# A down projection with two kinds of row-block pairs: the order in which its work is issued is written out and pinned

## The chip, the cores and the metric

The kernel runs on one core of one Trainium2 chip. The metric is the device time of one execution in microseconds (us). Three runs of the kernel before took 1710.01, 1710.61 and 1711.74 us; the median is 1710.61 us.

In the profile, PE is TensorE (matmuls; PEld its weight loads), DVE is VectorE, ACT is ScalarE, POOL is GpSimd and SP is SyncE, whose queue issues nearly all the DMAs. L102 is line 102 of the kernel.

## The reference, cut to what matters

One layer over 256 positions of width 2048: three gated attention branches, an output projection and a residual add, then a gated MLP. Only the end of the MLP is touched by the change:

```python
    h2 = _rmsnorm(x, ffn_norm)
    u = _causal_dwconv(h2 @ w_up, conv_w, conv_b)
    g, val = jnp.split(u, 2, axis=-1)
    return x + (jax.nn.silu(g) * val) @ w_down
```

`w_down` is 5504 x 2048 in float32, that is 43 row blocks of 128 rows.

## The kernel before, in words

**Float32 out of two parts.** Every matmul operand is split into a high part (an ACT copy into fp32r) and a low part (DVE: the value minus its high part). A product of two operands is three matmuls: high by high, high by low, low by high. Activations are split once; weights are split as they stream in. A weight tile is `raw` (128 x 1024, 512 KB, one DMA on SP's queue, 4 buffers), its high part is `whi` and its low part `wlo` (3 buffers each). `w_raw` (L155 holds its DMA) takes the tiles in one fixed order, `w_tiles` (L165, L166) splits them.

**The down projection.** The output is made in two halves of 1024 columns. In a half there are four cells: two blocks of 128 positions (`tt`) by two blocks of 512 columns (`h`). Two PSUM tiles `cc[0]` and `cc[1]` (pool `pj`, 2 buffers) hold the cells of one `tt` each. Row blocks are multiplied in two ways:

- A single block (`eight`): per cell three matmuls of 512 columns, so 12 matmuls.
- A pair of blocks (`seven`): the four blocks of a 2 x 2 product are made from seven products instead of eight (Strassen's scheme in Winograd's form), so 21 matmuls. Three of the products go straight into cells; the other four accumulate in four PSUM tiles `p1`, `p5`, `p6`, `p7` over all such pairs of the half. On the weight side a pair needs four differences of 128 x 512 (DVE, into `t`, L892 to L895), the high and low part of the first block's first 512 columns (`ha`, `la`), those of the second block (`hb`, `lb`), and the high and low parts of the four differences (`thl`, two at a time, L900 and L901). On the activation side three sums per pair (`sx`) are made while the up projection runs. The pairs that are done so are listed in `SEVEN`: 2, 3, 5, 7, 8, 10, 12, 13, 15, 17 (pair p holds blocks 2p and 2p+1); the other 23 blocks are single.

After the last pair of `SEVEN`, `gather` (L917 to L927) adds the four accumulators into `e`, the half's residual rows, which were loaded from DRAM (L861): one ACT copy of `p6` and seven DVE additions. The last three blocks (`TAIL`) are held until all three are split, and are then multiplied cell by cell; after each cell `store` (L929 to L932) adds it into `e` on DVE and issues the DMA to the output, on SP's queue for `tt` = 0 and on ACT's for `tt` = 1. In the last half the last cell is done in two pieces of 256 columns.

**What sets the order.** The engines run in parallel and each runs its own instructions in the order in which they were issued to it. That order isn't the order of the program text: a scheduler at build time picks, for every engine, the instruction with the highest priority among those that it takes to be ready. Priority is the order of the text, but instructions inside `tc.high_priority()` (the splits and differences of the weights) come ahead. Buffers of a pool are given out by it too; an instruction that needs a buffer waits for the last reader of its previous content.

Of the kernel before, what the change touches and what calls it, by code (L numbers as in the profile page):

```python
# [11 lines left out]
F32 = mybir.dt.float32  # L12
F32R = mybir.dt.float32r
# [27 lines left out]

SEVEN = (2, 3, 5, 7, 8, 10, 12, 13, 15, 17)
TAIL = 3


# [41 lines left out]
def hybrid_block(ctx: ExitStack, tc: tile.TileContext, x, xT, mem, memT, pos, inv, prm, gqk, bg, wts, out):  # L89
# [712 lines left out]
    with ExitStack() as fctx:  # L802
# [2 lines left out]
        sx = ap_.tile([P, len(SEVEN), 3, 2, P], F32R, name="sx")  # L805
        uctx = ExitStack()
        up = uctx.enter_context(tc.tile_pool(name="up", bufs=2))
        for c0 in range(0, NFF, 2):
            nb = min(2, NFF - c0)
            conv = []  # L810
            for half in range(2):
                ps = proj_cols(x2c, "up", KD, half * DFF + c0 * P, nb * P)
                u = up.tile([P, 2, T + 2], F32, name="u", bufs=3)
                nc.gpsimd.memset(u[:, :, 0:2], 0.0)
                uv = u[:, :nb, 2:]
                nc.scalar.activation(uv, ps[:, :nb, 1, :], AF.Copy)
# [31 lines left out]
        def mm3(o, l, r, start, stop):  # L848

            mm(o, l[0], r[0], start, False)  # L850
            mm(o, l[0], r[1], False, False)
            mm(o, l[1], r[0], False, stop)

        def hl(t):
            return t[:, 0, :], t[:, 1, :]

        for c0 in range(0, D, 1024):
            last = c0 + 1024 == D
            e = dn.tile([P, 2, 2, 512], F32, name="e")
            for tt in range(2):  # L860
                nc.sync.dma_start(e[:, tt], x2d[tt * P:(tt + 1) * P, c0:c0 + 1024])  # L861
            cc = [pj.tile([P, 2, 512], F32, name="pj") for _ in range(2)]
            p1, p5, p6, p7 = (pa.tile([P, 512], F32, name=nm, bufs=nb) for nm, nb in
                              (("t", 1), ("s", 2), ("s", 2), ("o", 1)))
            begun = set()

            def add(key, o, l, r, stop):
                mm3(o, l, r, key not in begun, stop)
                begun.add(key)

            def eight(k, hi, lo, cells, cols=(0, 512)):
                for tt, h in cells:
                    r = tuple(w[:, h * 512 + cols[0]:h * 512 + cols[1]] for w in (hi, lo))
                    add((tt, h), cc[tt][:, h, cols[0]:cols[1]], hl(fc[:, k, :, tt * P:(tt + 1) * P]), r,
                        k == NFF - 1)

            cells = [(tt, h) for tt in range(2) for h in range(2)]

            def seven(p):
                a, b = 2 * p, 2 * p + 1  # L880
                i, end = SEVEN.index(p), p == SEVEN[-1]
                ra, rb = (w_raw("down", k, c0, 1024)[0] for k in (a, b))
# [6 lines left out]
                with tc.high_priority():  # L889
                    nc.scalar.activation(ha[:, :512], b11, AF.Copy)  # L890
                    nc.scalar.activation(hb, rb, AF.Copy)
                    nc.vector.tensor_sub(t[:, 0], b12, b11)  # L892
                    nc.vector.tensor_sub(t[:, 1], b12, b22)  # L893
                    nc.vector.tensor_sub(t[:, 2], b22, t[:, 0])
                    nc.vector.tensor_sub(t[:, 3], b21, t[:, 2])  # L895
                    nc.vector.tensor_sub(la[:, :512], b11, ha[:, :512].bitcast(F32))
                    nc.vector.tensor_sub(lb, rb, hb.bitcast(F32))
                    for q in range(2):
                        th, tl = tq[:, 0, 2 * q:2 * q + 2], tq[:, 1, 2 * q:2 * q + 2]
                        nc.scalar.activation(th, t[:, 2 * q:2 * q + 2], AF.Copy)  # L900
                        nc.vector.tensor_sub(tl, t[:, 2 * q:2 * q + 2], th.bitcast(F32))  # L901
                step()
# [6 lines left out]
                add("p1", p1, a11, w11, end)  # L909
                add((0, 0), cc[0][:, 0], a12, w21, False)  # L910
                add((0, 1), cc[0][:, 1], s4, w22, False)
                add("p5", p5, s1, w1, end)
                add("p7", p7, s3, w3, end)
                add("p6", p6, s2, w2, end)
                add((1, 0), cc[1][:, 0], a22, w4, False)

            def gather():  # L917

                u = wraw.tile([P, 1024], F32, name="raw")[:, :512]
                nc.vector.tensor_add(e[:, 0, 0], e[:, 0, 0], p1)  # L920
                nc.scalar.activation(u, p6, AF.Copy)
                nc.vector.tensor_add(u, u, p1)
                for tt in range(2):
                    nc.vector.tensor_add(e[:, tt, 1], e[:, tt, 1], p5)
                nc.vector.tensor_add(e[:, 0, 1], e[:, 0, 1], u)
                nc.vector.tensor_add(u, u, p7)
                nc.vector.tensor_add(e[:, 1], e[:, 1], u.unsqueeze(1).to_broadcast([P, 2, 512]))  # L927

            def store(tt, a, b):  # L929
                d = e[:, tt].rearrange("p h n -> p (h n)")[:, a:b]  # L930
                nc.vector.tensor_add(d, d, cc[tt].rearrange("p h n -> p (h n)")[:, a:b])  # L931
                (nc.sync, nc.scalar)[tt].dma_start(out[tt * P:(tt + 1) * P, c0 + a:c0 + b], d)  # L932

            for p in range((NFF - TAIL) // 2):
                if p in SEVEN:
                    seven(p)
                    if p == SEVEN[-1]:
                        gather()
                else:
                    for k, hi, lo in w_tiles("down", 2 * p + 2, c0, 1024, 2 * p):  # L940
                        eight(k, hi, lo, cells)
            rest = list(w_tiles("down", NFF, c0, 1024, NFF - TAIL))
            for tt, h in cells:
                if last and (tt, h) == cells[-1]:
                    for a in (0, 256):
                        for k, hi, lo in rest:
                            eight(k, hi, lo, [(tt, h)], (a, a + 256))
                        store(tt, h * 512 + a, h * 512 + a + 256)
                else:
                    for k, hi, lo in rest:  # L950
                        eight(k, hi, lo, [(tt, h)])
                    store(tt, h * 512, h * 512 + 512)


_ORDER = ["x", "xT", "mem", "memT", "pos", "inv", "prm", "gqk", "bg", "wts"]
# [39 lines left out]
```

## Time and profile before

| | |
|---|---|
| time, median of 3 runs | 1710.61 us (1710.01 to 1711.74) |
| profiled execution | 1710.57 us, its span 1708.8 us |
| DVE, ACT, POOL busy | 1175.5, 897.0, 6.9 us |
| DMA | 332.78 MB, mean 195 GB/s |
| weight tiles | 586 DMAs of up to 512 KB on SP's queue, 3.4 us to landing (median of the 581 full ones) |
| down projection, first to last matmul | 1457.47 to 1705.4 us of the span |
| splitting a tile of 1024 columns | ACT 1057 ns, DVE 1220 ns (means of 549) |

How to read it: "busy" is the time in which an engine worked, as a share of the span. A line of a group names the source line, engine, operation, what it writes and reads, and the count; behind the bar come busy time and the mean of one, and behind a second bar the idle time just before them with what ended it. In the timeline a row has start, duration, engine, line, operation and tiles; brackets at its end give the idle time before it and what released it. Rows that follow each other may be merged (x2, x3).

### The profile page before, as it was taken

The page shows a single profiled execution, that of the slowest core. Times are in us where ns is not written, and L with a number is a line of the kernel's source. Part 1 is how long each engine was busy: PE and PEld are TensorE (multiplying, and loading weights), DVE is VectorE, ACT ScalarE, POOL GpSimd, SP SyncE. Part 2 cuts the span into 40 slices and gives each one's busy share as a digit, 9 for nine tenths or more (in the row PEclk, how much of TensorE's full clock was granted, in tenths as well). Part 3 has the DMA queues.
Part 4 walks back from the last instruction along what each step waited for, and adds up shares of the span by engine and source line. Part 5 has one row for each costly group of instructions (what it writes and reads, how often), then busy time and mean ns, then how long its engine had stood idle before and what let it go on. Part 6 is the DMA issues. An engine that isn't in the chain of part 4 may idle for free.

```text
span 1708.8 us, 22370 instructions
## 1 busy us (share of the span) xinstructions
PE 1682.8 (98%) x8349; PEld 1419.3 (83%) x8349; DVE 1175.5 (69%) x1770; ACT 897.0 (52%) x1197; POOL 6.9 (0%) x58
## 2 busy tenths in 40 slices
PE   8999999999999999999999999999999999998997
PEld 6888889888888888888888888888888888786786
DVE  6686866686554455555555577878777777996895
ACT  6555554445444477544444555555555555563552
POOL 0000000000000000000000000000000000000000
PEclk9999999999999999999999999999999999999999
DMA  9955445555565655576667655655555555665663
GB/s 324 299 186 187 147 153 183 179 184 180 185 197 187 194 173 173 182 214 207 197 211 221 217 188 190 192 187 194 187 191 191 187 195 185 210 209 166 219 206 111
DMA packets 98669, 332.78 MB, mean 195 GB/s; under 512 B 11008, under 2 KB 15744, under 8 KB 98560
## 3 DMA queue, kind: packets, MB, share of 16 engines
q1 hardware_dynamic: 97696, 330.29, 59.5%
q8 instruction: 65, 1.06, 0.2%
q10 hardware_dynamic: 864, 1.06, 0.2%
q14 instruction: 44, 0.36, 0.1%
HBM read 327.11 MB, written 4.19 MB: 194 GB/s over the span
## 4 chain that ended last, share of the span: by engine, by line
PE 94%; DVE 3%; DMA 2%; issue 1%; ACT 0%; SPq 0%; DVEq 0%; ACTq 0%
PE pj L102 88%; PE s L102 3%; PE o L102 2%; DMA raw<-in_wts 1%; DVE wlo L166 1%; PE t L102 1%; DMA out<-e 0%; ACT whi L165 0%; PE t L560 0%; PE t L781 0%; DVE t L893 0%; DVE e L931 0%; PE t L755 0%; PE t L331 0%; PE t L682 0%
## 5 line engine op out<-in xcount | busy, mean ns | idle before, releaser
L166 DVE TENSOR_TENSOR wlo<-raw,whi 128x1024 fp32r<-128x1024 f32 (+1 forms) x549 | 669.0, 1220 | 453.4 <-ACT whi L165 452.4
L165 ACT ACTIVATE whi<-raw 128x1024 fp32r<-128x1024 f32 (+1 forms) x549 | 579.0, 1057 | 686.1 <-PE pj L102 539.7
L102 PE MATMUL pj<-whi,xc 128*128 128x512 f32 (+2 forms) x1536 | 481.1, 387 | 0.5 <-DVE xc L198 0.5
L102 PE MATMUL pj<-x2c,whi 128*128 128x512 f32 x1376 | 477.4, 391 | 0.0
L102 PE MATMUL pj<-x2c,wlo 128*128 128x256 f32 x1376 | 385.5, 280 | 0.0
L102 PEld LDWEIGHTS pj<-whi,xc 128*128 128x128 f32 x1536 | 285.2, 188 | 55.2 <-DVE xc L198 1.0
L102 PEld LDWEIGHTS pj<-x2c,whi 128*128 128x128 f32 x1376 | 257.3, 187 | 56.3
L102 PE MATMUL pj<-wlo,xc 128*128 128x512 f32 (+2 forms) x768 | 293.3, 382 | 0.0
L102 PEld LDWEIGHTS pj<-x2c,wlo 128*128 128x128 f32 x1376 | 260.1, 189 | 0.0
L102 PEld LDWEIGHTS pj<-wlo,xc 128*128 128x128 f32 x768 | 144.6, 188 | 25.9
L102 PE MATMUL pj<-whi,fc 128*128 128x512 f32 (+1 forms) x454 | 149.5, 397 | 6.6 <-DVE e L931 2.8
L102 PEld LDWEIGHTS pj<-whi,fc 128*128 128x128 f32 x454 | 86.5, 192 | 28.2 <-DVE e L931 4.4
L102 PE MATMUL pj<-wlo,fc 128*128 128x512 f32 (+1 forms) x227 | 90.8, 400 | 8.7 <-DVE wlo L166 7.4
L102 PE MATMUL pj<-xc,whi 128*128 128x512 f32 x256 | 88.9, 394 | 0.0
L102 PE MATMUL pj<-whi,mc 128*128 128x512 f32 x256 | 82.9, 402 | 5.6 <-ACT whi L165 5.6
L102 PE MATMUL pj<-whi,mg 128*128 128x512 f32 x256 | 81.1, 392 | 0.0
L102 PE MATMUL pj<-xc,wlo 128*128 128x256 f32 x256 | 70.9, 277 | 0.0
L102 PEld LDWEIGHTS pj<-whi,mc 128*128 128x128 f32 x256 | 49.6, 194 | 16.6 <-ACT whi L165 6.3
L900 ACT ACTIVATE thl<-t 128x1024 fp32r<-128x1024 f32 x40 | 42.2, 1056 | 39.2 <-DVE t L893 32.5
L102 PEld LDWEIGHTS pj<-wlo,fc 128*128 128x128 f32 x227 | 43.9, 193 | 20.6 <-DVE wlo L166 9.5
L102 PEld LDWEIGHTS pj<-xc,whi 128*128 128x128 f32 x256 | 48.0, 188 | 11.1
L102 PEld LDWEIGHTS pj<-whi,mg 128*128 128x128 f32 x256 | 48.1, 188 | 9.8
(255 smaller groups left out, 1709.7 us busy)
## 6 DMA issues: line engine op xcount, KB each, us to landing
raw<-in_wts SPq DMA_DIRECT2D x581, 512.0 KB, 3.4
th<-in_bg SPq DMA_DIRECT2D x24, 256.0 KB, 5.4
raw<-in_wts SPq DMA_DIRECT2D x5, 492.0 KB, 3.3
nat_rows<-in_mem SPq DMA_DIRECT2D x4, 512.0 KB, 6.5
nat_rows<-in_x SPq DMA_DIRECT2D x4, 512.0 KB, 6.3
xf<-in_xT SPq DMA_DIRECT2D x4, 512.0 KB, 5.6
xrow<-in_x SPq DMA_DIRECT2D x8, 256.0 KB, 5.1
x2d<-xrow SPq DMA_DIRECT2D x8, 256.0 KB, 4.5
```

The costliest lines, as they stand in the source:

```text
L102: nc.tensor.matmul(o, l, r, start=start, stop=stop, skip_group_check=True)
L165: nc.scalar.activation(hi[:, :kn * n], raw[:, :kn * n], AF.Copy)
L166: nc.vector.tensor_sub(lo[:, :kn * n], raw[:, :kn * n], hi[:, :kn * n].bitcast(F32))
L900: nc.scalar.activation(th, t[:, 2 * q:2 * q + 2], AF.Copy)
```

## The change

`SEVEN` becomes the nine odd pairs 1, 3, ..., 17, so that a pair of single blocks and a `seven` pair alternate; blocks 36 to 42 are single. All matmuls, ACT and DVE instructions of the down projection are issued through `keep` (`tc.keep_in_program_order`), which pins each behind everything that the program text has before it on its engine. DMAs aren't pinned. `high_priority` and the calls of `step()` go from this stage. The gather becomes the generator `share`, whose five steps are taken one behind each block from block 38 on, with a buffer `u3` of its own. Only the last half holds three blocks and goes cell by cell; the first half multiplies all its blocks in the usual way, and its results are added and stored at the start of the second half, all stores on SP's queue. The second half's residual rows are loaded behind its block 9. The first two tiles of the down projection are prepared before the last up block's convolution. In `seven`, `la` and `lb` are now made before the third and fourth difference.

```diff
-SEVEN = (2, 3, 5, 7, 8, 10, 12, 13, 15, 17)
+SEVEN = (1, 3, 5, 7, 9, 11, 13, 15, 17)
...
+        keep = tc.keep_in_program_order
+
+        def prepare(k, c0):
+            raw, _ = w_raw("down", k, c0, 1024)
+            hi = whl.tile([P, 1024], F32R, name="whi")
+            lo = whl.tile([P, 1024], F32R, name="wlo")
+            keep(nc.scalar.activation(hi, raw, AF.Copy))
+            keep(nc.vector.tensor_sub(lo, raw, hi.bitcast(F32)))
+            return k, hi, lo
+
...
                 ps = proj_cols(x2c, "up", KD, half * DFF + c0 * P, nb * P)
+                if nb == 1 and half == 1:
+                    ready = [prepare(k, 0) for k in range(2)]
...
+        def share(e, p1, p5, p6, p7):
+
+            u = dn.tile([P, 512], F32, name="u3")
+            keep(nc.scalar.activation(u, p6, AF.Copy))
+            yield
+            keep(nc.vector.tensor_add(e[:, 0, 0], e[:, 0, 0], p1))
+            keep(nc.vector.tensor_add(u, u, p1))
+            yield
+            for tt in range(2):
+                keep(nc.vector.tensor_add(e[:, tt, 1], e[:, tt, 1], p5))
+            yield
+            keep(nc.vector.tensor_add(e[:, 0, 1], e[:, 0, 1], u))
+            keep(nc.vector.tensor_add(u, u, p7))
+            yield
+            keep(nc.vector.tensor_add(e[:, 1], e[:, 1], u.unsqueeze(1).to_broadcast([P, 2, 512])))
...
+                high(ha[:, :512], b11)
+                high(hb, rb)
+                sub(t[:, 0], b12, b11)
+                sub(t[:, 1], b12, b22)
+                sub(la[:, :512], b11, ha[:, :512].bitcast(F32))
+                sub(lb, rb, hb.bitcast(F32))
+                sub(t[:, 2], b22, t[:, 0])
+                sub(t[:, 3], b21, t[:, 2])
+                for q in range(2):
+                    th, tl = tq[:, 0, 2 * q:2 * q + 2], tq[:, 1, 2 * q:2 * q + 2]
+                    high(th, t[:, 2 * q:2 * q + 2])
+                    sub(tl, t[:, 2 * q:2 * q + 2], th.bitcast(F32))
...
+        e, before = residual(0), None
+        for c0 in range(0, D, 1024):
+            if before is not None:
+                ready = [prepare(0, c0)]
+                for tt, h in cells:
+                    result(*before, tt, h * 512, h * 512 + 512)
+            half, shares, held = Half(c0), None, []
+            for p in range(NFF // 2 + 1):
+                if p in SEVEN:
+                    half.seven(p)
+                    continue
+                for k in range(2 * p, min(2 * p + 2, NFF)):
+                    item = ready.pop(0) if ready else prepare(k, c0)
+                    assert item[0] == k
+                    if k < NFF - TAIL or c0 + 1024 < D:
+                        half.eight(item, cells)
+                    else:
+                        held.append(item)
+                    if k == 2 * SEVEN[-1] + 4:
+                        shares = share(e, *half.p)
+                    if shares is not None:
+                        next(shares, None)
+                    if before is not None and k == 1:
+                        for tt, h in cells:
+                            store(before[0], 0, tt, h * 512, h * 512 + 512, nc.sync)
+                    if before is not None and k == 9:
+                        e = residual(c0)
+            before = e, half.cc
+        for tt, h in cells:
+            for a in ((0, 256) if (tt, h) == cells[-1] else (0,)):
+                n = 256 if (tt, h) == cells[-1] else 512
+                for item in held:
+                    half.eight(item, [(tt, h)], (a, a + n))
+                result(e, half.cc, tt, h * 512 + a, h * 512 + a + n)
+                store(e, D - 1024, tt, h * 512 + a, h * 512 + a + n, (nc.sync, nc.scalar)[tt])
```

More of the change, by code (lines that the diff above doesn't have):

```diff
@@ L846, in hybrid_block, with residual @@
         turn_ = [0]
[L848 to L852, printed above, removed]
+        cells = [(tt, h) for tt in range(2) for h in range(2)]
         def hl(t):
             return t[:, 0, :], t[:, 1, :]
-        for c0 in range(0, D, 1024):
-            last = c0 + 1024 == D
+        def residual(c0):
             e = dn.tile([P, 2, 2, 512], F32, name="e")
@@ L861, in hybrid_block @@
                 nc.sync.dma_start(e[:, tt], x2d[tt * P:(tt + 1) * P, c0:c0 + 1024])
[L862 to L872, printed above, removed]
+            return e
@@ new lines, in flat, with result, store, __init__ @@
+        def flat(e, tt, a, b):
+            return e[:, tt].rearrange("p h n -> p (h n)")[:, a:b]
+        def result(e, cc, tt, a, b):
+            d = flat(e, tt, a, b)
+            keep(nc.vector.tensor_add(d, d, cc[tt].rearrange("p h n -> p (h n)")[:, a:b]))
+        def store(e, c0, tt, a, b, queue):
+            queue.dma_start(out[tt * P:(tt + 1) * P, c0 + a:c0 + b], flat(e, tt, a, b))
+        class Half:
+            def __init__(self, c0):
+                self.c0, self.begun = c0, set()
+                self.cc = [pj.tile([P, 2, 512], F32, name="pj") for _ in range(2)]
+                self.p = [pa.tile([P, 512], F32, name=nm, bufs=nb) for nm, nb in
+                          (("t", 1), ("s", 2), ("s", 2), ("o", 1))]
+            def add(self, key, o, l, r, stop):
+                first = key not in self.begun
+                self.begun.add(key)
+                for i, (a, b) in enumerate(((0, 0), (0, 1), (1, 0))):
+                    keep(nc.tensor.matmul(o, l[a], r[b], start=first and i == 0, stop=stop and i == 2,
+                                          skip_group_check=True))
+            def eight(self, item, which, cols=(0, 512)):
+                k, hi, lo = item
+                for tt, h in which:
@@ L873, in eight, with seven @@
                     r = tuple(w[:, h * 512 + cols[0]:h * 512 + cols[1]] for w in (hi, lo))
[L874 to L879, printed above, removed]
+                    self.add((tt, h), self.cc[tt][:, h, cols[0]:cols[1]], hl(fc[:, k, :, tt * P:(tt + 1) * P]), r,
+                             k == NFF - 1)
+            def seven(self, p):
@@ L880, in seven @@
                 a, b = 2 * p, 2 * p + 1
                 i, end = SEVEN.index(p), p == SEVEN[-1]
-                ra, rb = (w_raw("down", k, c0, 1024)[0] for k in (a, b))
+                ra, rb = (w_raw("down", k, self.c0, 1024)[0] for k in (a, b))
                 ha, hb = (whl.tile([P, 1024], F32R, name="whi") for _ in range(2))
@@ L888, in seven, with high, sub @@
                 b11, b12, b21, b22 = ra[:, :512], ra[:, 512:], rb[:, :512], rb[:, 512:]
[L889 to L902, printed above, removed]
+                def high(dst, src):
+                    keep(nc.scalar.activation(dst, src, AF.Copy))
+                def sub(dst, x_, y_):
+                    keep(nc.vector.tensor_sub(dst, x_, y_))
+                high(ha[:, :512], b11)
[10 more added lines that the diff above has]
+                    sub(tl, t[:, 2 * q:2 * q + 2], th.bitcast(F32))
                 w11 = ha[:, :512], la[:, :512]
@@ L908, in seven @@
                 a12, a22 = (hl(fc[:, b, :, tt * P:(tt + 1) * P]) for tt in range(2))
[L909 to L934, printed above, removed]
-                if p in SEVEN:
[L936 to L952, printed above, removed]
+                p1, p5, p6, p7 = self.p
@@ new lines, in seven @@
+                self.add("p1", p1, a11, w11, end)
+                self.add((0, 0), self.cc[0][:, 0], a12, w21, False)
+                self.add((0, 1), self.cc[0][:, 1], s4, w22, False)
+                self.add("p5", p5, s1, w1, end)
+                self.add("p7", p7, s3, w3, end)
+                self.add("p6", p6, s2, w2, end)
+                self.add((1, 0), self.cc[1][:, 0], a22, w4, False)
+        e, before = residual(0), None
[6 more added lines that the diff above has]
+            for p in range(NFF // 2 + 1):
+                if p in SEVEN:
+                    half.seven(p)
[17 more added lines that the diff above has]
+            before = e, half.cc
```

## The prediction

> **What bounds the kernel now.** I read the page first, then the windows view cut by stage, then the timeline of the engines where a stage loses time, then the waits of SP's queue.
>
> ```profile
> span 1708.8 us, 22370 instructions
> PE 1682.8 (98%) x8349; PEld 1419.3 (83%) x8349; DVE 1175.5 (69%) x1770; ACT 897.0 (52%) x1197; POOL 6.9 (0%) x58
> PE 94%; DVE 3%; DMA 2%; issue 1%; ACT 0%; SPq 0%; DVEq 0%; ACTq 0%
> ...
> 1457.40:1480.00 22.60, 21.02 (x89) 1.00 0.56 183
> 1480.00:1551.00 71.00, 71.00 (x313) 1.00 0.63 209
> 1551.00:1606.00 55.00, 46.51 (x181) 0.94 0.62 204
> 1606.00:1677.00 71.00, 70.83 (x312) 1.00 0.58 190
> 1677.00:1694.80 17.80, 13.89 (x50) 0.81 0.34 119
> 1694.80:1708.80 14.00, 9.08 (x45) 0.94 0.23 75
> ```
>
> TensorE (PE) is the bound: busy for 98% of the span, and 94% of the chain that ended last. The windows (stretch, its length, PE busy time, matmuls, granted clock) hold the down projection, 1457.4 us to the end. Inside a half, PE has no idle time (71.00 of 71, 70.83 of 71). It idles 8.5 us at the change of halves (55.00 less 46.51), 3.9 us near the end of the second, 4.9 us in the tail, 1.6 us at the start. The change touches only this stage, so I price it as PE's matmuls plus PE's waits.
>
> ```profile
> 1457.47 0.39 PE L102 MATMUL pj<-whi,fc 128*128 128x512 f32 x1
> ...
> 1692.07 1.06 ACT L165 ACTIVATE whi<-raw 128x1024 fp32r<-128x1024 f32 x1 [1.66 <-PE pj L102]
> ...
> 1694.79 1.06 ACT L165 ACTIVATE whi<-raw 128x1024 fp32r<-128x1024 f32 x1 [1.66 <-PE pj L102]
> ...
> 1695.88 1.23 DVE L166 TENSOR_TENSOR wlo<-raw,whi 128x1024 fp32r<-128x1024 f32 x1 [1.49 <-ACT whi L165]
> ...
> 1697.16 0.50 PE L102 MATMUL pj<-wlo,fc 128*128 128x512 f32 x1
> ...
> 1700.60 0.61 PE L102 MATMUL pj<-whi,fc 128*128 128x512 f32 x2
> ...
> 1702.37 0.39 PE L102 MATMUL pj<-whi,fc 128*128 128x256 f32 x1 [1.15 <-DVE e L931]
> ...
> 1704.21 0.39 PE L102 MATMUL pj<-whi,fc 128*128 128x256 f32 x1 [0.51 <-DVE e L931]
> ...
> 1705.27 0.28 PE L102 MATMUL pj<-whi,fc 128*128 128x256 f32 x1
> ```
>
> The first two ACT rows are the high parts of two row blocks; each waited until PE left an old block, so they lie one block apart: 2.72 us for 12 matmuls, 0.2267 us each. The program has 972 full-width matmuls here (20 new pairs of 21, 46 single blocks of 12): 220.4 us of work. From 1457.47 to the end of the last one, 1705.38, are 247.9 us. So 27.5 us are lost, and these are all that the change can win.
>
> ```profile
> 1551.47 0.60 ACT L921 ACTIVATE raw<-s 128x512 f32<-128x512 f32 x1 [5.69 <-PE s L102]
> 1551.97 2.94 ACT L165 ACTIVATE whi<-raw 128x1024 fp32r<-128x1024 f32 x3
> ...
> 1553.07 0.73 PE L102 MATMUL pj<-whi,fc 128*128 128x512 f32 x2 [0.95 <-ACT whi L165]
> 1556.76 0.66 PE L102 MATMUL pj<-wlo,fc 128*128 128x512 f32 x1 [2.96 <-DVE wlo L166]
> 1557.22 1.06 PE L102 MATMUL pj<-whi,fc 128*128 128x512 f32 x2
> ...
> 1562.59 0.62 PE L102 MATMUL pj<-whi,fc 128*128 128x512 f32 x2
> ...
> 1576.75 0.50 PE L102 MATMUL pj<-whi,fc 128*128 128x512 f32 x1 [1.15 <-DVE e L931]
> 1577.09 0.39 PE L102 MATMUL pj<-wlo,fc 128*128 128x512 f32 x1
> ...
> 1598.76 0.50 PE L102 MATMUL pj<-whi,fc 128*128 128x512 f32 x1 [1.61 <-ACT whi L891]
> 1600.06 0.51 PE L102 MATMUL pj<-wlo,fc 128*128 128x512 f32 x1 [0.79 <-DVE wlo L897]
> ...
> 1597.65 1.06 ACT L891 ACTIVATE whi<-raw 128x1024 fp32r<-128x1024 f32 x1 [5.77 <-DMA raw<-in_wts]
> ...
> SPq L932 <- DVE e L931: 21.0, 4, 14.3
> SPq L861 <- DMA out<-e: 7.4, 1, 7.4
> ```
>
> Three things lose it. First, the gather: ACT stood 5.69 us at its copy of p6 (L921) with three high parts queued behind, and DVE gave its gather adds the turn before the low parts; PE waited 0.95 and 2.96 us, and then ran pairs of matmuls in 1.06 us instead of 0.62, the clock being halved. The second half has the same (clock 0.81 in 1677 to 1694.8). Second, the three held blocks that end each half: they fill all three weight slots, and PE waits for the adds into e (1.15 us). Third, SP: a store waited up to 14.3 us for e and a residual load 7.4 us for the stores, with weight loads behind them on the same queue; a raw came 5.77 us late and PE stood 1.61 and 0.79 us.
>
> **The change, part by part.** *Matmuls.* 18 new pairs of 21 and 50 blocks of 12 make 978: six more, +1.4 us, 221.7 us in all. The sequence is one eight-pair (5.44 us), one new pair (4.76 us): 10.2 us.
>
> *Gather and middle.* The copy of p6 now comes after the high part of block 38, over two blocks after p6 is complete, so ACT doesn't stand there. The eight vector operations go into five steps, one behind each of the seven single blocks' low parts, at most 1.2 us in 2.72 us of PE: hidden by PE; without that cover they cost what they cost now. Block 42 is multiplied before any result is added, and the next half's block 0 is prepared ahead of the four adds. PE's next matmul needs both adds into the first PSUM tile.
>
> ```profile
> 1499.66 0.68 DVE L894 TENSOR_TENSOR t<-raw,t 128x512 f32<-128x512 f32 x1
> 1500.27 1.22 DVE L897 TENSOR_TENSOR wlo<-raw,whi 128x1024 fp32r<-128x1024 f32 x1
> 1501.40 1.21 DVE L166 TENSOR_TENSOR wlo<-raw,whi 128x1024 fp32r<-128x1024 f32 x1
> ...
> 1507.88 0.68 DVE L893 TENSOR_TENSOR t<-raw 128x512 f32<-128x512 f32 x1
> ...
> 1508.59 1.07 ACT L900 ACTIVATE thl<-t 128x1024 fp32r<-128x1024 f32 x1 [3.56 <-DVE t L893]
> ```
>
> DVE starts the next instruction 0.61 us after a 512-wide one and 1.13 us after a 1024-wide one; a 512-wide result is used 0.71 us after its start, a 1024-wide one after 1.28 us (1695.88 to 1697.16), a high part after 1.09 us (1694.79 to 1695.88). Block 42's second quarter ends 1.36 us before the half does; 0.2 us to the read and two adds of 0.61 end some 0.1 to 0.3 us after it. I take 0.3 us, bounds 0 and the 4.6 us of idle time (8.5 less the gather's 3.9) that this place has now.
>
> *Stores and residual on SP.* All four stores of the first half go to SP, traced behind block 1, the load of e behind block 9. Behind them are raws of blocks needed three tiles later. If they wait in the order in which DVE makes e, nothing is late; the row of 7.4 us is the other end. I take 0.5 us.
>
> *The pinned order in a half.* The preparation of a new pair is now one fixed chain on DVE: two differences, la, lb, two differences, two low parts. lb and hb sit in the slot of the eight-block E0 one block before. From E0's end: hb 1.09; lb starts there, and takes 1.13; t2 and t3 1.2, with 0.1 between dependent ones; first low part starts at 3.55 and is ready at 4.83. PE reaches it after E1 (12 matmuls), nine of the pair and one more: 22 x 0.2267 = 4.99. It is 0.16 us in time. The second low part is ready at 6.06, wanted at 28 x 0.2267 = 6.35. lb is ready at 2.37, wanted at 3.63. DVE's whole work in the 10.2 us is five of 0.61 and five of 1.13, 8.7 us. So PE stays fed, closely. Lateness would cost 0.11 us more each time (a matmul after a wait takes 0.34 instead of 0.23: 1576.75 to 1577.09). I take 1.0 us over the 17 pairs behind the first; bounds 0 and 10 us (half a microsecond late each).
>
> *Start.*
>
> ```profile
> 1458.57 0.36 ACT L816 ACTIVATE u<-pj 128x256 f32<-128x256 f32 x1
> ...
> 1463.15 1.23 DVE L166 TENSOR_TENSOR wlo<-raw,whi 128x1024 fp32r<-128x1024 f32 x1 [0.23 <-ACT whi L165]
> ...
> 1464.89 0.42 DVE L198 TENSOR_TENSOR fc<-cv,fc 128x256 fp32r<-128x256 f32 x1
> ```
>
> The first new pair comes after two blocks instead of four, at 1457.47 + 5.44 = 1462.91, and DVE may not begin it before the up stage's last split (L198). That took 6.32 us from L816, 1.74 of it work that now comes later (1463.15 to 1464.89). L816 can start near 1457.6, so L198 starts at 1462.2, the differences at 1462.65, and la is ready at 1464.6 (wanted 1463.14: 1.4 late), then lb 0.4 and the first low part 0.95 late: with three restarts 3.1 us. If L198 stays at 1464.89, 2.7 more. The idle time there now is 1.6 us.
>
> *Tail.* Block 42's low part comes 2.37 us after block 39 ends (1694.79 to 1697.16), and PE wants it as eighth matmul, at 1.59: 0.8 us. DVE then has the last gather step, 1.13, before the first add; PE's second cell writes the same tile and waits about 1.2 us (bounds 0, if two cells of one tile don't hold each other up, and 1.3: 1700.83 to 1702.37 less a matmul). The last cell waits 0.95 and its second piece 0.67, as now. With restarts 4.0 us.
>
> *Sum.* 1457.47 + 221.7 + 3.1 + 0.3 + 0.5 + 1.0 + 4.0 = 1688.1 for PE's end. The last add and store take 3.4 us as now (1705.38 to 1708.8): span 1691.5. The profiled execution took 1710.57, 1.77 over its span, and is 0.04 under the median of 1710.61: **1693.2 us**, 1.0% faster.
>
> *The clock.*
>
> ```profile
> 1590.00:1606.00 16.00, 13.34 (x50) 0.89 0.79 272
> ```
>
> After waits of 1.61 and 0.79 us this window's clock is 0.89, so waits well under 3 us brought it down. By these rows the start's 2.8 us of waits within 5 us could halve the clock once more; the stretch at half clock after 1556.76 cost about 1.7 us. [...] I leave it out of the sum and have 1.7 us in the range.
>
> **The rivals.** *Small waits at every pair.* The fixed order keeps the slots busy but each pair is 0.5 us late: 17 x 0.61 = 10.4 us in place of 1.0: 1702.6 us. For it: 0.16 us of slack rests on five hops. Against it: 71.00 of 71 us busy with pairs closer together.
>
> *The order isn't really fixed.* Matmuls, ACT and DVE are pinned, DMAs aren't. If SP again has stores and the load of e ahead of needed raws, the middle keeps its 4.6 us of idle time and a half-clock stretch of 1.7: 1693.2 + 6.3 - 0.8 = 1698.7 us.
>
> *Slower.* Today PE may take whichever product is ready; pinned, it stands at the first one that isn't. If lb, stuck for its slot, holds back both differences and both low parts by 1.7 us more than the chain above, each pair costs 1.5 + 0.11: 17 x 1.61 = 27.4 in place of 1.0, 1719.6 us. It decides against the change from about 1.1 us a pair (18.4 / 17). For it: ACT's row at 1551.47 shows what one early instruction in a queue does. Against it: today's halves run the same operations through the same three slots with 71.00 of 71 us busy. [...]
>
> *No difference*: several of these at once give back 17 us.
>
> **How the numbers follow.** Forecast 0.57, small waits 0.18, order not fixed 0.12, slower 0.09, no difference 0.04. Faster by over 0.2% (about what a measurement can tell) holds the first three: 0.87. Low end: without the 1.5 us of small terms, the tail's 1.2 and 2 us of the start, 1688.5. High end past the first two rivals: 1704.
>
> **What would show it.** Right: PE busy through 1551 to 1606 at full clock; no ACT wait at p6; last half-clock stretches gone; PE waits only near 1463 to 1468 and in the tail. Wrong: PE waits for a low part of thl once every 10.2 us (first and third rival), a raw landing late after the half (second).

## The result and the profile after

Over 15 runs each the changed kernel took 1698.26 us (median) and the kernel before 1710.61 us. The ratio is 0.9929, 95% interval 0.9908 to 0.995: faster by 0.7%, 12.4 us, where 1693.2 us was forecast, within the range of 1688.5 to 1704. Two of the 15 executions (3095.7 and 2085.6 us) ran at a mean clock of 0.78 and 0.75, and are left out of the ratio.

The page of the changed kernel, one execution of 1706.59 us:

```profile
span 1704.9 us, 22359 instructions
PE 1689.1 (99%) x8355; PEld 1418.8 (83%) x8355; DVE 1167.5 (68%) x1753; ACT 890.4 (52%) x1192; POOL 6.9 (0%) x58
PE 98%; DVE 1%; DMA 0%; ACT 0%; issue 0%; SPq 0%; DVEq 0%; ACTq 0%
```

PE's share of the chain that ended last rose from 94% to 98%. The windows view of the down projection, cut where this execution loses time (stretch, length, PE busy time, matmuls, clock, DMA share and GB/s):

```profile
1467.30:1483.00 15.70, 13.66 (x58) 1.00 0.64 200
1483.00:1565.00 82.00, 82.00 (x357) 1.00 0.60 201
1565.00:1600.00 35.00, 34.89 (x154) 1.00 0.80 263
1600.00:1685.00 85.00, 85.00 (x370) 1.00 0.60 200
1685.00:1690.80 5.80, 4.93 (x21) 1.00 0.00 0
1690.80:1704.90 14.10, 8.60 (x36) 0.88 0.20 74
```

The change of halves lost 8.5 us of PE's time before, in a stretch of 55 us; it loses 0.1 now (1565 to 1600), at full clock. Near the end of the second half 3.9 us were lost; 0.9 are left (1685 to 1690.8), the tail's first wait. The idle time that is left lies at the start and in the tail. This view doesn't show short losses: the 82.00 us out of 82 hold eight pairs that each lost 0.16 us, which only the distances between the starts of matmuls show (*The pinned order in a half*, below).

But the span is only 3.9 us shorter, and the stage begins 10 us later. The view of one tile (count, shortest, median and longest in ns, first and last start) for the up projection's matmuls, first in the kernel before, then in this profile of the changed kernel, then in a second profile of the same changed kernel (named "again" below):

```profile
L102 PE MATMUL pj<-x2c,whi x1376: 389/391/478, 978.9 to 1457.1; 128*128 128x512 f32 x197
```

```profile
L102 PE MATMUL pj<-x2c,whi x1376: 389/398/476, 979.8 to 1467.0; 128*128 128x512 f32 x197
...
L910 PE MATMUL pj<-whi,fc x478: 279/389/794, 1467.4 to 1701.3; 128*128 128x512 f32 x156, 128*128 128x256 f32 x4
```

```profile
L102 PE MATMUL pj<-x2c,whi x1376: 389/391/478, 979.3 to 1457.5; 128*128 128x512 f32 x197
...
L910 PE MATMUL pj<-whi,fc x478: 278/389/504, 1457.8 to 1690.3; 128*128 128x512 f32 x156, 128*128 128x256 f32 x4
```

By these rows, which hold every second matmul, the up projection took 487.2 us in one execution and 478.2 in the other, of one and the same program (487.4 and 478.4 over all its matmuls); the last section returns to it. So whole times mislead by 9 us here, and from now on the measure is the down projection from its first matmul to its last: 247.9 us before, 234.05 in the first profile of the changed kernel, 232.6 in the second. The forecast had 230.6.

### The profile page after: what moved, and what is told of

Read it like the earlier page. It is cut to its first block, busy times and chain, and to the rows that moved or that the text cites. A ratio compares the mean times of both kernels' runs of the same rounds, so it can differ in the third digit from the quotient of the medians.

```text
span 1704.9 us, 22359 instructions
## 1 busy us (share of the span) xinstructions
PE 1689.1 (99%) x8355; PEld 1418.8 (83%) x8355; DVE 1167.5 (68%) x1753; ACT 890.4 (52%) x1192; POOL 6.9 (0%) x58
## 4 chain that ended last, share of the span: by engine, by line
PE 98%; DVE 1%; DMA 0%; ACT 0%; issue 0%; SPq 0%; DVEq 0%; ACTq 0%
PE pj L102 81%; PE pj L910 10%; PE s L102 2%; PE s L910 2%; PE o L102 1%; PE o L910 1%; PE t L910 1%; DMA raw<-in_wts 0%; PE t L560 0%; PE t L781 0%; PE t L755 0%; PE t L331 0%; PE t L682 0%; DVE t L935 0%; DVE e L891 0%
## 5 line engine op out<-in xcount | busy, mean ns | idle before, releaser
L166 DVE TENSOR_TENSOR wlo<-raw,whi 128x1024 fp32r<-128x1024 f32 (+2 forms) x503 | 613.9, 1220 | 441.0 <-ACT whi L165 438.8
L165 ACT ACTIVATE whi<-raw 128x1024 fp32r<-128x1024 f32 (+2 forms) x503 | 531.5, 1057 | 644.5 <-PE pj L102 509.1
L102 PE MATMUL pj<-x2c,whi 128*128 128x512 f32 x1376 | 486.4, 399 | 0.0
L910 PE MATMUL pj<-whi,fc 128*128 128x512 f32 (+1 forms) x478 | 154.0, 390 | 2.4 <-DVE e L891 2.3
L910 PEld LDWEIGHTS pj<-whi,fc 128*128 128x128 f32 x478 | 90.2, 189 | 22.5 <-DVE e L891 3.4
L815 DVE TENSOR_TENSOR wlo<-raw,whi 128x1024 fp32r<-128x1024 f32 x50 | 59.3, 1220 | 6.3 <-ACT whi L814 6.3
L814 ACT ACTIVATE whi<-raw 128x1024 fp32r<-128x1024 f32 x50 | 50.5, 1047 | 20.2 <-PE pj L910 17.9
L932 ACT ACTIVATE whi<-raw 128x512 fp32r<-128x512 f32 (+1 forms) x36 | 30.1, 838 | 55.7 <-PE pj L910 53.1
```

What stands on the lines that cost most here:

```text
L102: nc.tensor.matmul(o, l, r, start=start, stop=stop, skip_group_check=True)
L165: nc.scalar.activation(hi[:, :kn * n], raw[:, :kn * n], AF.Copy)
L166: nc.vector.tensor_sub(lo[:, :kn * n], raw[:, :kn * n], hi[:, :kn * n].bitcast(F32))
L814: keep(nc.scalar.activation(hi, raw, AF.Copy))
L815: keep(nc.vector.tensor_sub(lo, raw, hi.bitcast(F32)))
L910: keep(nc.tensor.matmul(o, l[a], r[b], start=first and i == 0, stop=stop and i == 2, skip_group_check=True))
```

## The experiments

Times of runs with an interval are against the kernel before. Where "down projection" stands with a number of two decimals, it runs from the first matmul's start to the last one's in the trace, plus 0.11 us (half of 0.2267) for the last, as the 247.9 us of the prediction do; the end that the last row shows is 0.17 us later. Sums of lost time are the distances between the starts of neighbouring matmuls less 0.2267 us, added up where they are clearly longer. The start of the stage is its first 22 us, which hold two pairs, the tail what comes after 218 us, the middle the rest. Runs without an interval were executed once, so that small differences between them are differences of single profiles.

**again.** The changed kernel, unchanged.

> The changed kernel once more. In its first profile the up projection took 487.4 us from its first to its last matmul (978.4 in the kernel before: 478.4), although nothing in it was changed but its last tile; the down projection took 234.05 us. My theory: the pace of the up projection differs from execution to execution, the down projection's doesn't. Then the down projection again takes 234 us, within 0.5, and the up projection may come out at 478 or 488 us; with 478 the span is 1695 us. The rival: the changed program is always slower in the up projection; then it takes 488 us here too, and in all variants that keep the change.

Median 1695.94 us, ratio 0.9911 (0.9882 to 0.994). The up projection took 478.4 us and the down projection 232.57: my theory held for the first, and the down projection was 1.5 us shorter than in the first profile, which is more than the 0.5 I allowed. The timeline of the tail shows why. First profile of the changed kernel:

```profile
1689.83 1.22 DVE L884 TENSOR_TENSOR e<-e,u 128x1024 f32<-128x1024 f32 x1
1690.96 0.68 DVE L891 TENSOR_TENSOR e<-e,pj 128x512 f32<-128x512 f32 x1
...
1689.97 0.50 PE L910 MATMUL pj<-wlo,fc 128*128 128x512 f32 x1 [0.77 <-DVE wlo L815]
...
1691.70 0.79 PE L910 MATMUL pj<-whi,fc 128*128 128x512 f32 x1 [1.00 <-DVE e L891]
...
1692.72 1.05 PE L910 MATMUL pj<-whi,fc 128*128 128x512 f32 x2
...
1698.40 0.39 PE L910 MATMUL pj<-whi,fc 128*128 128x256 f32 x1 [0.78 <-DVE e L891]
```

The second:

```profile
1682.21 0.50 PE L910 MATMUL pj<-whi,fc 128*128 128x512 f32 x1 [1.00 <-DVE e L891]
...
1682.79 0.63 PE L910 MATMUL pj<-whi,fc 128*128 128x512 f32 x2
```

The same waits, 0.77 and 1.00 us, and behind them matmul pairs of 1.05 us in one and 0.63 in the other: the clock halved only once. The last section shows what was different.

**early_differences.**

```diff
                 sub(t[:, 1], b12, b22)
-                sub(la[:, :512], b11, ha[:, :512].bitcast(F32))
-                sub(lb, rb, hb.bitcast(F32))
                 sub(t[:, 2], b22, t[:, 0])
                 sub(t[:, 3], b21, t[:, 2])
+                sub(la[:, :512], b11, ha[:, :512].bitcast(F32))
+                sub(lb, rb, hb.bitcast(F32))
```

> The changed kernel with all four differences of a pair ahead of la and lb on DVE (the order before). My theory: each pair waits because two differences stand behind lb, which waits for its slot; the first low part was ready 4.83 us after the eight-block's end as worked out, but PE wants it at its weight load, 0.2 us ahead of the matmul. With the differences done before, the low part is ready at about 3.5 us, and the 17 waits with their restarts (0.16 us each) go: the down projection takes 231.3 us instead of 234.05. The rival: the extra 0.05 and 0.11 us come from the switch to another accumulator and other weights; then nothing changes (234 us).

One pair in the changed kernel, from the timeline:

```profile
1493.83 1.06 ACT L932 ACTIVATE whi<-raw 128x1024 fp32r<-128x1024 f32 x1 [3.23 <-PE pj L910]
...
1494.92 1.23 DVE L935 TENSOR_TENSOR wlo<-raw,whi 128x1024 fp32r<-128x1024 f32 x1 [1.41 <-ACT whi L932]
...
1496.06 1.41 DVE L935 TENSOR_TENSOR t<-raw,t 128x512 f32<-128x512 f32 x2
...
1496.35 0.39 PE L910 MATMUL t<-whi,fc 128*128 128x512 f32 x1
...
1497.39 2.44 DVE L935 TENSOR_TENSOR thl<-t,thl 128x1024 fp32r<-128x1024 f32 x2
...
1498.39 1.01 PE L910 MATMUL s<-thl,sx 128*128 128x512 f32 x3
...
1498.66 0.30 PEld L910 LDWEIGHTS s<-thl,sx 128*128 128x128 f32 x2 [0.31 <-DVE thl L935]
```

From hb (1493.83) over lb, two differences and the low part to the weight load that waited for it (1498.66) are 4.83 us, as worked out. With the differences first:

```profile
1487.21 1.23 DVE L935 TENSOR_TENSOR wlo<-raw,whi 128x1024 fp32r<-128x1024 f32 x1 [1.30 <-ACT whi L932]
...
1488.35 2.35 DVE L935 TENSOR_TENSOR thl<-t,thl 128x1024 fp32r<-128x1024 f32 x2
...
1490.45 0.64 PEld L910 LDWEIGHTS s<-thl,sx 128*128 128x128 f32 x3
...
1466.89 0.79 PE L910 MATMUL t<-wlo,fc 128*128 128x512 f32 x1 [2.39 <-DVE wlo L935]
```

The low parts follow lb directly, and the weight load doesn't wait. All pair waits but one are gone: 2.9 us of lost time in the middle of the stage became 0.7. The rival is out. Still the down projection took 232.55 us, not 231.3: at the start la now comes behind two more differences, PE waited 2.39 us there (last row), and the clock halved behind it and again in the tail (mean clock of the run 0.997, against 1.0 in "again"). Median 1695.67 us, ratio 0.9907 (0.9878 to 0.9937).

**tail_by_turns.**

```diff
-        for tt, h in cells:
+        for tt, h in [(0, 0), (1, 0), (0, 1), (1, 1)]:
             for a in ((0, 256) if (tt, h) == cells[-1] else (0,)):
```

> The changed kernel with the last four cells in the order (0,0), (1,0), (0,1), (1,1), so that no cell follows one of its own PSUM tile. My theory: a cell waits for the add of the other cell of its tile; with the turns the waits before the second cell (1.0 us of idle time) and before the fourth (0.8 us) go, and the stretch at half clock (2 us) with them, since only the 0.8 us wait for the last low part is left ahead of it: the down projection takes about 229.7 us instead of 234.05. The rival: each cell waits for the add of the cell before it, whichever tile that is: 234 us. If only the waits go and the clock still halves, it is 231.7.

All of the tail's waits on PE:

```profile
1689.20 0.50 PE L910 MATMUL pj<-wlo,fc 128*128 128x512 f32 x1 [0.77 <-DVE wlo L815]
...
1695.66 0.39 PE L910 MATMUL pj<-whi,fc 128*128 128x256 f32 x1 [0.52 <-DVE e L891]
```

The waits of 1.00 and 0.78 us are gone, and the clock stayed up (1.0 in the mean of the run). The time lost in the tail fell from 3.9 us (in "again") to 1.7, the down projection took 230.74 us: 1.8 us less than "again", 3.3 less than the first profile. My figure of 229.7 was 1 us too low; of the rivals, the one by which every cell waits for the one before is out. A cell waits for the add of the cell in its own PSUM tile. Median 1694.4 us, ratio 0.9909 (0.9879 to 0.9939).

**no_pins.**

```diff
-        keep = tc.keep_in_program_order
+        keep = lambda ins: ins
```

> The changed kernel without pinning: keep returns the instruction and adds nothing, so the scheduler orders all engines again, by the order of the text. My theory: the gain comes from the restructured ends of the halves (no copy of p6 in ACT's way, one held group fewer), not from the pins; the down projection then takes 232 to 238 us. The rival: the pins bring the gain; without them the scheduler interleaves the products as before and loses at the ends as before: 243 us or more.

```profile
L910 PE MATMUL pj<-whi,fc x478: 274/389/498, 1458.6 to 1686.7; 128*128 128x512 f32 x156, 128*128 128x256 f32 x4
```

The down projection took 228.25 us, less than any figure I gave, and 4.3 us less than with the pins. Median 1693.46 us, ratio 0.9898 (0.9863 to 0.9933). The gain doesn't come from the pins; they cost, 4.3 us in these two profiles and 2.5 in the medians of four executions each (1695.94 and 1693.46 us). Of the 9.8 us lost with pins 5.9 are left: 1.65 at the start (with pins 3.0), 2.0 in the middle (2.9), 2.2 in the tail (3.9).

**before_odd_pairs.**

```diff
-SEVEN = (2, 3, 5, 7, 8, 10, 12, 13, 15, 17)
+SEVEN = (1, 3, 5, 7, 9, 11, 13, 15, 17)
```

in the kernel before, and nothing else.

> The kernel before with the list of pairs alone changed to the nine odd ones. Its down projection took 247.9 us from first to last matmul, with ten pairs. My theory: the time is lost at the ends of the halves (gather, held blocks, stores on SP), not in the mix of pairs; six more matmuls add 1.4 us: 246 to 250 us, with PE waits behind pair 17 in both halves as before. The rival: alternation itself brings the gain: 237 us or less.

```profile
L102 PE MATMUL pj<-whi,fc x478: 274/389/632, 1466.1 to 1708.5; 128*128 128x512 f32 x156, 128*128 128x256 f32 x4
```

242.48 us, below my range and above the rival's figure. The losses behind the gather's copy stayed (1.11 and 3.13 us in both halves, as in the kernel before). Between the first half's gather and the next pairs the lost time fell from 7.9 to 2.8 us, and the second half's stretch at half clock, 6.83 us in the kernel before, was half as long (mean clock of the run 0.997, against 0.996). So under the old structure the list of pairs isn't without effect: the order that the scheduler makes of it around the change of halves came out better. Which instruction's place did it wasn't followed.

**gather_at_once.** The changed kernel, its five steps directly behind the last pair.

```diff
                     half.seven(p)
+                    if p == SEVEN[-1]:
+                        for _ in share(e, *half.p):
+                            pass
                     continue
...
-                    if k == 2 * SEVEN[-1] + 4:
-                        shares = share(e, *half.p)
```

> The changed kernel with all five steps of the gather taken directly behind the last pair, pinned, not one behind each later block. The changed kernel's down projection takes 232.6 us when the clock isn't halved in its tail. My theory: the high part of block 36 stands behind the copy of p6 on ACT, and its low part behind seven vector operations; PE waits 5 to 6 us per half and then runs at half clock for about 3.4 us, 1.7 us more: 243 to 248 us. The rival: the steps are hidden wherever they stand, since three tiles are prepared ahead: 232 to 234 us.

ACT, DVE and PE behind the last pair of the first half:

```profile
1562.17 0.60 ACT L873 ACTIVATE u<-s 128x512 f32<-128x512 f32 x1 [2.24 <-PE s L910]
1562.66 2.94 ACT L814 ACTIVATE whi<-raw 128x1024 fp32r<-128x1024 f32 x3
...
1566.11 1.22 DVE L884 TENSOR_TENSOR e<-e,u 128x1024 f32<-128x1024 f32 x1
1567.25 3.49 DVE L815 TENSOR_TENSOR wlo<-raw,whi 128x1024 fp32r<-128x1024 f32 x3
...
1563.76 0.50 PE L910 MATMUL pj<-whi,fc 128*128 128x512 f32 x1 [0.95 <-ACT whi L814]
1568.52 0.79 PE L910 MATMUL pj<-wlo,fc 128*128 128x512 f32 x1 [4.26 <-DVE wlo L815]
1569.11 1.05 PE L910 MATMUL pj<-whi,fc 128*128 128x512 f32 x2
```

This is the picture of the kernel before: the copy of p6, three high parts behind it, the gather's adds, and only then the low parts; PE waits 0.95 and 4.26 us (before: 0.95 and 2.96) and goes on at half clock. The second half did the same. The down projection took 249.84 us, 17.3 more than "again", more than the 10 to 15 expected, and more than the kernel before, with about two thirds of it at the gathers' waits and the rest at half clock behind them and in the tail (mean clock of the run 0.996): under the pins, spreading the gather is worth more than the whole gain of 15.3 us in this stage.

**hold_both.** The changed kernel, with three blocks held at the end of the first half too.

```diff
-                    if k < NFF - TAIL or c0 + 1024 < D:
+                    if k < NFF - TAIL:
...
+            if c0 + 1024 < D:
+                for tt, h in cells:
+                    for item in held:
+                        half.eight(item, [(tt, h)])
             before = e, half.cc
```

> The changed kernel with the last three blocks held and multiplied cell by cell in both halves, where it does so in the last half only; results are still added after all four cells. My theory: PE waits 1.0 us for the last low part, and about 1.0 us for the next half's first low part, whose slot is only free when the last cell has used it; with restarts 2 to 3 us: 234.6 to 235.6 us instead of 232.6. The rival: the held blocks cost nothing without the adds between the cells: 232.6 us; or they cost all that the kernel before lost there, 5 us and more.

```profile
1581.53 2.00 ACT L814 ACTIVATE whi<-raw 128x1024 fp32r<-128x1024 f32 x2 [6.90 <-PE pj L910]
...
1582.62 1.23 DVE L815 TENSOR_TENSOR wlo<-raw,whi 128x1024 fp32r<-128x1024 f32 x1 [5.60 <-ACT whi L814]
1583.76 2.47 DVE L891 TENSOR_TENSOR e<-e,pj 128x512 f32<-128x512 f32 x4
...
1585.18 0.47 PE L910 MATMUL pj<-whi,fc 128*128 128x512 f32 x1 [2.34 <-DVE e L891]
```

236.02 us, 3.5 more than "again", where 2 to 3 were expected. The slot is late as I said (ACT waits 6.90 us for PE), but PE doesn't wait for the low part: it waits for the adds into e, which stand behind that low part on DVE because the text has them so, 2.34 us. I had missed that a pinned wait passes itself on to work that was ready.

**no_pins_old_pairs.** The kernel of no_pins with the old ten pairs.

```diff
-SEVEN = (1, 3, 5, 7, 9, 11, 13, 15, 17)
+SEVEN = (2, 3, 5, 7, 8, 10, 12, 13, 15, 17)
```

> The changed kernel without pins, which took 228.25 us in the down projection, with the ten pairs of the kernel before (2, 3, 5, 7, 8, 10, 12, 13, 15, 17) in place of the nine odd ones. My theory: the scheduler feeds neighbouring pairs too, as it did inside the halves of the kernel before, and six matmuls fewer save 1.4 us: 226.5 to 228 us. The rival: neighbouring pairs (7 and 8, 12 and 13) starve PE, since DVE needs 6.4 us for a pair that PE does in 4.8: 230 us or more.

```profile
L910 PE MATMUL pj<-whi,fc x454: 274/389/499, 1459.3 to 1687.6; 128*128 128x512 f32 x148, 128*128 128x256 f32 x4
```

228.40 us, against 228.25 with the odd pairs, just outside what I expected: six matmuls fewer (1.4 us) and 1.4 us more of waits in all (0.9 fewer at the start, 2.3 more in the middle). Once the ends are right, the choice of pairs makes no difference between these two profiles. So all of the change's gain in this stage, and 4 us beyond it, come from what else it changed: 247.9 to 228.4 us. That is the structure of the halves' ends, and also the high priority that went; no run separates the two, or the parts of the structure, without pins.

**free_pe and pin_pe.** Pins on ACT and DVE only, and on the matmuls only.

```diff
-                    keep(nc.tensor.matmul(o, l[a], r[b], start=first and i == 0, stop=stop and i == 2,
+                    free(nc.tensor.matmul(o, l[a], r[b], start=first and i == 0, stop=stop and i == 2,
```

In pin_pe it is the other way round: every other `keep` becomes `free`, with `free = lambda ins: ins`.

> The changed kernel with its pins on ACT and DVE only; the matmuls are ordered by the scheduler. All pins together cost 4.3 us of the down projection (232.57 against 228.25 us). My theory: what costs is PE standing at the first product that isn't ready (0.16 us at each pair, 2.8 us at the start, 1.2 and 0.9 us in the tail); free matmuls can go round it, so this takes 228 to 230 us. The rival: the fixed chain on DVE is what costs; then it stays at 232 us, and pins on PE alone cost nothing.

> The changed kernel with its pins on the matmuls only; ACT and DVE are ordered by the scheduler. My theory: the scheduler puts the differences ahead of lb and so the pair waits go (2.8 us), but the waits at the start and in the tail stay: 229.5 to 231 us in the down projection, the waits at 1.2 and 0.9 us in the tail as in the changed kernel. The rival: the pins on DVE are all that costs: 228.3 us.

The matmul row of free_pe's down projection, and its weight loads' waits:

```profile
L911 PE MATMUL pj<-whi,fc x478: 278/389/504, 1457.2 to 1688.1; 128*128 128x512 f32 x156, 128*128 128x256 f32 x4
...
PEld s L911 <- DVE thl L936: 5.5, 18, 0.3
```

231.01 us, between theory and rival: the tail got back 1.5 us and the start 0.3, but all 18 pairs still wait for the low part of thl. Nothing else was put in front of it; why the scheduler didn't, I can't say. pin_pe took 235.42 us, more than with all pins: a stretch at half clock fell in at its start (mean clock of the run 0.997), and it lost 4.3 us in the middle, with waits up to 1.2. So my theory that PE's pins are what costs holds for the tail alone, the rival's for the pairs, and a fixed PE under a free DVE is the worst of the four (all pinned, nothing, all but PE, PE alone) in these profiles.

**no_pins_by_turns.** The edits of no_pins and tail_by_turns together.

> The changed kernel without pins and with the last four cells in the order (0,0), (1,0), (0,1), (1,1): the two best edits together. My theory: without pins one wait for an add into the same PSUM tile was left before the last cell (1.3 us); with the turns it goes, and the down projection takes 226.9 us instead of 228.25; with the up projection at 478.4 us the time is about 1690.5 us. The rival: the scheduler had already taken the cells by turns, and nothing is left to gain: 228.3 us, 1692 us.

1692.3 us in the median, ratio 0.9897 (0.9881 to 0.9914): 1.0% faster than the kernel before, and not to be told apart from no_pins. The tail lost 0.7 us instead of 2.2, as expected of the turns. But the down projection took 229.79 us in the profile, not 226.9: behind the change of halves a raw came late,

```profile
1584.22 0.69 DVE L935 TENSOR_TENSOR t<-raw 128x512 f32<-128x512 f32 x1 [3.16 <-DMA raw<-in_wts]
...
1588.57 0.59 PE L910 MATMUL pj<-wlo,fc 128*128 128x512 f32 x1 [1.06 <-DVE wlo L935]
1588.96 1.05 PE L910 MATMUL pj<-whi,fc 128*128 128x512 f32 x2
```

and PE lost 0.8 and 1.3 us there and then ran at half clock. Without pins that place stays open to such a wait; with them it cost PE at most 0.5 us (*SP*, below).

**rhythm.** The changed kernel with a transpose that nothing uses behind every step of the up projection.

```diff
             split(fc[:, c0:c0 + nb], v_)
+            brk = pa.tile([P, 512], F32, name="t")
+            nc.tensor.transpose(brk[:, :P], v_[:, 0, :P], ident)
```

> The changed kernel with one extra transpose on PE behind each of the 22 steps of the up projection (work that nothing uses), to break the sequence of its matmuls. In ten profiles the up projection took either 478.4 or 487.4 us, nothing between; in the first all pairs of matmuls lie 0.347 us apart, in the second three pairs take 1.060 us. My theory: this is a rhythm of weight loads and matmuls that keeps itself once it is set by nanoseconds at the start; broken 22 times, it is set anew, and both paces (11.09 and 11.31 us for 64 matmuls) show up in one execution. The rival: the pace is a state of the execution: one pace throughout, whichever.

All stretches between the breaks went at 11.09 us for 64 matmuls; each break cost about 0.28 us, and the up projection took 484.7 us. The two paces that my theory wanted in one execution didn't show up; one pace throughout is what the rival said. It stays inconclusive, since one execution that may have begun in the faster pace can't tell whether a break ever sets it anew.

## Why the prediction was right, and where its sum was off

*What bounds the kernel* was read rightly: all that the change won in the stage was PE's waits and its half-clock stretches.

*Gather.* Right in mechanism, shown by gather_at_once, though the five steps hold seven vector additions and one ACT copy, not eight vector operations, and stand behind five blocks, not seven. *Middle* (the change of halves): 0.3 us forecast, 0.35 measured. *SP*: 0.5 forecast, 0 to 0.5 measured. The prediction's row of 14.3 us was misread: that store was issued at 1698.64 us, in the tail, with no weight load behind it; at the change of halves the stores before waited 1.2 and 2.8 us. The load of e still waits for the stores, but

```profile
SPq L867 <- DMA out<-e: 2.5, 1, 2.5
...
1595.09 0.64 ACT L932 ACTIVATE whi<-raw 128x512 fp32r<-128x512 f32 x1 [2.55 <-DMA raw<-in_wts]
```

2.5 us instead of 7.4. A raw did land late behind it: ACT waited 2.55 us for it in the first profile (second row). PE lost 0.05 us by it there, nothing in "again", and 0.5 us at the same place in tail_by_turns and gather_at_once. So the sign of the rival in which the order isn't really fixed was there, at 0 to 0.5 us instead of its 6.3; no_pins_by_turns shows that it was a real danger.

*Start*: 3.1 us forecast, 2.9 measured (the 3.0 above has the second pair's 0.16 in it). *Tail*: 4.0 forecast; 3.9 in "again", and 5.4 in the first profile, where the clock halved. I had priced that for the start only, at 1.7 us, and in the range, not in the sum: that the start would keep its clock was an estimate of mine that no trace of the kernel before showed. It did keep it: in the first profile PE was busy for 2.16 us of 1473.14 to 1476.55 and for 2.62 of the 3.41 us behind that, at a clock of 1.00, and the fall came at the tail.

*The pinned order in a half* is the step that failed. The chain of 4.83 us was right, but the time at which PE wants it wasn't. The pair's first matmul starts at 1496.35, so the block E0 had ended 2.72 us before, at 1493.63; hb starts at 1493.83. I had taken the start of the ACT instruction that waits for PE as the end of PE's block; it comes 0.2 us after it, as the read of PSUM by DVE does (in the kernel before the last matmul ends at 1705.38 and the last add starts at 1705.59), where I did count 0.2. So the 0.16 us of slack were a lateness of 0.05, and every pair behind the first lost 0.05 and the restart's 0.11 (the starts of its matmuls at 1498.39, 1498.66 and 1499.00 lie 0.275 and 0.338 us apart): 17 pairs, 2.7 us, in place of 1.0. What was expected of early_differences puts the 0.2 us down to the weight load ahead of the matmul instead; both fit the loss, and no run separates them. It was the first rival's mechanism at a quarter of its price, and the sign that the prediction named for it, a wait for a low part of thl every 10.2 us, was there. The slower rival was never near: it needed 1.1 us a pair.

*Matmuls.* 221.7 us forecast; 232.57 less 9.84 of lost time leave 222.7 in "again": 0.7 us because matmuls stand a little over 0.2267 us apart behind restarts (0.232 in the mean of the 12 from 1682.55 to 1685.33), 0.3 because lost time is counted against 0.2267 us for the 256-wide ones too. In sum 222.7 + 2.9 + 2.7 + 0.35 + 3.9 = 232.6 us, 2.0 over the forecast of 230.6. The rest of the 5.1 us between 1693.2 and 1698.26 goes mostly with the two paces of the up projection, as far as the profiles show: 5 of the 13 executions that count took 1702.9 to 1707.0 us, 8 took 1695.3 to 1698.3, and the profiled one of the first group had the slower up projection. The median is the longest of the 8. The forecast had no term for the pace, so it was in part luck that the median fell within the range: three of the 13 lay above its end at 1704. In the kernel before, 3 of 15 runs lay near 1720 and 12 between 1708 and 1713.

What I had argued but the runs don't bear out: that the fixed order keeps PE fed is true, but it isn't what wins. Without pins the rest of the change wins about 19.5 us in the down projection, and the pins give back 4.3 of it.

## What to carry to other kernels

Look for instructions that wait for the bound engine's last result and stand ahead of its next operands in another engine's queue; spread such work over later tiles, and it costs little (232.57 us in this stage, against 249.84 with the gather at once). (Here the last step of the gather still stood ahead of the tail's first add, at 1689.83, and PE waited 1.00 us behind the two.) Pinning an order fixes what you saw, but it also turns each late operand into a wait and passes a wait on to ready work behind it (2.34 us in hold_both): price each pinned chain with every hop between engines, and try the same structure without the pins. Where a program has two paces in a stage that wasn't touched, compare the stage, not the whole time.

## What the runs showed of the hardware that was not expected

*Two paces of one matmul sequence.* The up projection alternates matmuls of 512 and 256 columns, each with its own weights. In eight of thirteen profiles without the extra transposes all pairs lay 0.347 us apart and the stage took 478.4 us from first to last matmul; in the other five, three pairs in turn took 0.350, 0.361 and 0.349 us, 1.9% more in all, and the stage took 487.4 us. Nothing lay between, and kernels before and after the change were among either, and the changed kernel itself was in both. The two go apart 1.5 us after the stage begins, by a few ns (two starts lie 0.118 us apart in the kernel before and 0.124 in the first profile). What decides it stays open.

*The clock halved on short waits, where they fell together.* In the first profile of the changed kernel 0.77 and 1.00 us of waits within 2.5 us, with matmuls between them, brought a stretch of half clock; the same waits in "again" did not. In the traces of the kernel before and of the first profile such a stretch within the down projection lasts 3.41 us or twice that, and its starts lie on a grid of this step: in the kernel before they come at 1556.94, 1601.31 and 1679.82 us, 44.37 and 78.51 us or 13 and 23 steps apart. The grid starts at another point of the program in each execution: counted from the stage's first matmul, its points lie 0.48 us past a whole number of steps in the kernel before, 2.36 in the first profile and 0.7 in "again". Cut at that grid, the first profile and then "again" (stretch, length, PE busy time, matmuls, clock, DMA share and GB/s):

```profile
1688.18:1691.59 3.41, 1.75 (x7) 1.00 0.00 0
1691.59:1695.00 3.41, 3.30 (x8) 0.50 0.20 77
```

```profile
1676.94:1680.35 3.41, 2.77 (x12) 1.00 0.00 0
1680.35:1683.76 3.41, 2.28 (x9) 1.00 0.20 77
```

In the first profile both waits fell almost wholly into one cell of the grid, and PE was busy for 0.51 of it; in "again" most of the first wait fell into the cell before, and PE was busy for 0.81 and 0.67 of the two. The kernel before, cut in the same way around its three falls:

```profile
1553.53:1556.94 3.41, 0.45 (x3) 1.00 0.14 19
1556.94:1560.35 3.41, 3.41 (x9) 0.50 0.88 275
1597.90:1601.31 3.41, 1.75 (x7) 1.00 0.85 290
1601.31:1604.72 3.41, 3.41 (x9) 0.50 0.72 241
1676.41:1679.82 3.41, 1.44 (x6) 1.00 0.00 0
1679.82:1686.65 6.83, 4.89 (x12) 0.50 0.70 230
```

PE was busy for 0.13, 0.51 and 0.42 of the cell ahead of each. Of the other cells at full clock that lie whole within the down projection, in these two traces, the emptiest held 0.63 (1473.14 to 1476.55 in the first profile), and no fall came behind it. What share between 0.51 and 0.63 would bring one isn't shown. In price: 1.5 us of the down projection (234.05 us in the first profile, 232.57 in "again").
